# A hybrid decoder step on one core: the searches of a sparse list emitted further apart, and more products of ones ahead of the first wide product

## The chip, the cores and the metric

One Trainium2 chip, one of its cores. The metric is the device time of one launch in microseconds, the median of several runs; lower is better.

## The reference

One inference step of one decoder layer, for a prompt of 512 rows and a sample of 8 sequences with 4 rows each (544 rows of 1024 in all):

```
u = rmsnorm(h, g1);  h = h + 0.5 * rmsnorm(swiglu(u, wg, wu, wd), g2)
u = rmsnorm(h, g3);  z, xbc, dt, q, k, v, qi, ki, wi, g_ssd, g_att = split(u @ w_in)
y_ssd = ssd_branch(z, xbc, dt, ...)          # 32 heads in 8 groups
y_att = attn(q, k, v, qi, ki, wi)            # each row over its own 256 keys
merged = sigmoid(g_ssd) * (y_ssd @ w_br_ssd) + sigmoid(g_att) * (y_att @ w_br_att)
h = h + rmsnorm(merged @ w_out, g4)
...                                          # cross-attention to a memory, second FFN
```

The sparse attention of a sample row scores 4100 keys (4096 of them in paged caches), takes the 256 best, gathers their key and value rows by the page table, and attends over these:

```
score = einsum('bth,bths->bts', wi, relu(dots));  _, sel = top_k(score, 256)
k_sel = pool_k[page_table[sel // 128], sel % 128]   # and v_sel
```

## The kernel before

All work runs on one core, in float32. A wide product multiplies a weight block of 128 columns by 544 rows; operands are split into a high and a low part (`wh`, `wl` of a weight, `uh`, `ul` of the rows), and `mm` (line 315 issues them) makes three products for each of 8 blocks of k. `weights` loads a raw weight half by DMA (`wr`, three buffers), copies the high part on ScalarE (line 275) and subtracts for the low part on VectorE, or for some weights on GpSimd (line 276). There are two buffers each of `wh` and `wl`.

The kernel is written as generators. `weave` runs several of them by a clock of its own: a generator yields a pair (cost, delay), the cost moves that clock on, and the generator is resumed when its delay is over. This sets the order in which instructions are emitted. The framework then schedules them: the order of emission is their priority, and within each engine an instruction that isn't ready lets others pass. So the order on an engine can differ from that in the code.

**The start.** `load_x` loads the first 256 rows, and `first_T` transposes them on TensorE (line 481) for k = 0 to 7, two blocks of 128 rows each. ScalarE and VectorE make `uh` and `ul` of them (lines 485 and 486), with the first weight halves of the first FFN in between. Behind the transposes of k = 1, 3 and 5 `idle` multiplies a tile of ones by itself into a spare PSUM tile (line 248): 2, 2 and 8 products that nobody reads. Each leaves two records in the trace. Then the first wide products follow (line 315, `pgh`).

**The sparse list.** `sample_lists` finds the threshold of each sample row's list by 16 rounds of comparing and counting on VectorE, makes running counts, and then looks up the places of the 256 entries: 32 searches, each a `max_index` of 8 wanted counts in a row of 1028 (line 1130). They write slices of one tile and depend on nothing that the other generators do. It is begun beside the prompt's attention, and what is left of it goes on in `ssd`:

```python
fs.after(chain(rounds, self.sample_select(), call(sel_ex.close), self.sample_att()))
```

Here `rounds` is `sample_lists`; `sample_select` turns the places into row numbers (VectorE, one product); `sample_att` gathers key and value rows by indirect DMAs on GpSimd's queue, attends in four steps of 8 rows, and stores each step's result (`yas` to `yatt_d`, line 1712).

Beside that chain `ssd` weaves two more generators. `fronts` makes, group by group, the projections of B, C and x with their convolution (`ssd_x`, lines 1324 to 1341) and of z (`ssd_z`, line 1300); for two groups it also makes a piece of the gates, whose low parts GpSimd computes. When all groups are through it waits for the flag `fs`, which the end of `sample_att` sets; then `att_in` loads the attention's result (`yat`, line 1722) and splits it into `uh` and `ul`, and `att_out` multiplies it by `w_br_att`. `tails` runs `ssd_y` for each group: the scan, the state, and at its end the norm of the group (`rms`). There a sum of squares (line 346) goes through a chain of small VectorE operations for the reciprocal root (lines 331 to 336) to a diagonal `zt` (lines 357 and 359), which TensorE spreads over the rows (`psr`, line 360). Group g of `fronts` waits until the tail of group g - 2 has been emitted.

When `tails` and the chain have ended, `conv_rows` and `merge` follow: `merge` loads the 16 blocks of the branch's result (`yt`, three buffers, line 1758), splits them into `yh` and `yl`, weaves this with the rest of `att_out`, and multiplies by `w_br_ssd`.

Of the kernel before, what the change touches and what calls it, by code (L numbers as in the profile page):

```python
# [168 lines left out]
class Net:  # L169
# [297 lines left out]
    def first_T(self):  # L467


        nc, I = self.nc, self.I  # L470
        q = self.row_squares(0, (0,))
        pss = []
        for k in range(8):
            if k == 4:
                self.weights(("ffn1", "g", 0), [I["ffn1_wg"][0][:, :256]], 8)
            if k % 2 == 0:
                ps = self.ps1("pgx")
                pss.append(ps)
            v = ps[:, k % 2 * 256:(k % 2 + 1) * 256]
            for i in range(2):  # L480
                nc.tensor.transpose(v[:, i * P:(i + 1) * P], self.xin[i][:, k, :], self.ident)
            if k in (1, 3, 5):
                self.idle(self.spare, 2 if k < 5 else 8)
            gk = self.g1[:, k:k + 1]
            nc.scalar.activation(self.uh[:, k, :HA], v, AF.Copy, scale=gk)
            nc.vector.scalar_tensor_tensor(self.ul[:, k, :HA], v, gk, self.uh[:, k, :HA].bitcast(F32), op0=ALU.mult, op1=ALU.subtract)
        self.weights(("ffn1", "u", 0), [I["ffn1_wu"][0][:, :256]], 8)
        for i in range(2, 4):
            nc.sync.dma_start(self.xin[i], I["x_prompt"][0, i * P:(i + 1) * P, :].rearrange("p (k d) -> p k d", k=8))
        nc.sync.dma_start(self.xin[4], I["x_sample"].rearrange("b t (k d) -> (b t) k d", k=8))  # L490
        for c, ps in enumerate(pss):
            (nc.vector.tensor_copy if c % 2 else nc.scalar.copy)(self.hT[:, 2 * c:2 * c + 2, :HA], ps.rearrange("p (k t) -> p k t", k=2))

        def rest():
            self.row_squares(0, (1,), q)
            yield from self.row_factor(q, 0)

        return rest()
# [557 lines left out]
    def sample_lists(self):  # L1056
# [71 lines left out]
        nc.vector.tensor_scalar(at, at, bg, None, op0=ALU.subtract)  # L1128
        for r in range(32):
            nc.vector.max_index(self.IX[:, r * 8:(r + 1) * 8], at[:, r * 8:(r + 1) * 8], S)  # L1130
            yield 0.0, 3.4


    def gates(self, x, cs, tile):
# [960 lines left out]
```

## Time and profile before

| | |
|---|---|
| median of 3 runs | 2186.69 us (2183.43 to 2188.44) |
| the profiled execution's own time | 2168.1 us |
| its span, first to last instruction | 2165.3 us |
| mean granted TensorE clock | 0.981 |
| TensorE busy | 97% of the span |
| VectorE busy | 61% |
| ScalarE busy | 44% |
| GpSimd busy | 17% |

The profiled execution is one of its own, and every row below is from it. Busy time of an engine is the time in which it had an instruction in work. PEclk is the share of TensorE's full clock that was granted: 1.00 is 2.4 GHz and 0.50 is 1.2 GHz, and a value in between is a mean over a stretch that saw both.

### The profile page before, as it was taken

To read this page: it belongs to the slowest core of one execution; us is meant where nothing else is said; L and a number is where in the kernel's file an instruction comes from. 1 tells how busy PE (TensorE), PEld (TensorE's weight loads), DVE (VectorE), ACT (ScalarE), POOL (GpSimd) and SP (SyncE) were. 2 spreads that over 40 slices of the span, in tenths; PEclk is the share of its full clock that TensorE was granted. 3 is DMA by queue.
4 is the path that set the end of the run, shared out by engine and by line. 5 is a ranking of instruction groups with operands and counts; after the bars stand their busy time and mean duration, and the time that the engine had idled before them with its cause. 6 is when DMAs were issued, how large, how long until landed. Compare 5 with 4: busy or idle time off the path is not lost.

```text
span 2165.3 us, 41287 instructions
## 1 busy us (share of the span) xinstructions
PE 2096.3 (97%) x16725; PEld 1963.0 (91%) x16725; DVE 1324.1 (61%) x2759; ACT 956.2 (44%) x1821; POOL 377.7 (17%) x413
## 2 busy tenths in 40 slices
PE   8999999999999999999999999999999989999998
PEld 8999999998878769988889899899987889999998
DVE  6543334466587889997877788544663575424455
ACT  6323345345444675544555455323545443222233
POOL 0000011032113212205555620001210210000011
PEclk9999999998999899999999999999999989999999
DMA  6424556356443223444666556554444433233243
GB/s 200 130 68 137 154 183 230 104 145 197 139 145 93 75 81 105 137 140 140 177 184 184 163 160 194 175 163 168 155 143 156 140 109 117 78 108 90 72 133 101
DMA packets 320106, 301.70 MB, mean 139 GB/s; under 512 B 25416, under 2 KB 290632, under 8 KB 318868
## 3 DMA queue, kind: packets, MB, share of 16 engines
q1 hardware_dynamic: 310508, 272.58, 41.0%
q0 software_dynamic: 8448, 25.18, 3.9%
q8 instruction: 131, 2.15, 0.4%
q10 hardware_dynamic: 960, 1.31, 0.2%
q14 instruction: 59, 0.48, 0.1%
HBM read 261.14 MB, written 37.35 MB: 138 GB/s over the span
## 4 chain that ended last, share of the span: by engine, by line
PE 77%; DVE 12%; DMA 4%; ACT 4%; issue 2%; POOL 0%; SPq 0%; DVEq 0%; ACTq 0%; POOLq 0%
PE pg L315 44%; PE pgh L315 17%; PE pmo L601 2%; DVE wl L276 2%; DVE gtm L1087 1%; ACT wh L275 1%; DMA abc<-ac_d 1%; DMA yt<-yssd_d 1%; DMA wr<-in_ffn_wg 1%; DMA wr<-in_ffn_wu 1%; PE ph L1448 1%; PE pmkT L1821 1%; PE pqk L1199 1%; PE pmo L1888 1%; PE pms L1877 1%
## 5 line engine op out<-in xcount | busy, mean ns | idle before, releaser
L275 ACT CAST wh<-wr 128x1024 fp32r<-128x1024 f32 (+3 forms) x362 | 342.2, 959 | 510.7 <-PE pg L315 237.3
L276 DVE TENSOR_TENSOR wl<-wr,wh 128x1024 fp32r<-128x1024 f32 (+3 forms) x338 | 377.3, 1128 | 210.6 <-ACT wh L275 206.2
L315 PE MATMUL pg<-uh,wh 128*128 128x256 f32 (+1 forms) x2336 | 501.1, 295 | 0.0
L315 PE MATMUL pg<-uh,wl 128*128 128x256 f32 (+1 forms) x2336 | 490.6, 290 | 0.0
L315 PE MATMUL pg<-ul,wh 128*128 128x256 f32 (+1 forms) x2336 | 489.7, 290 | 0.0
L315 PEld LDWEIGHTS pg<-uh,wh 128*128 128x128 f32 x2336 | 378.4, 190 | 19.4 <-issue 16.6
L315 PEld LDWEIGHTS pg<-ul,wh 128*128 128x128 f32 x2336 | 378.8, 190 | 3.0 <-issue 2.6
L315 PEld LDWEIGHTS pg<-uh,wl 128*128 128x128 f32 x2336 | 378.0, 189 | 1.3 <-issue 1.0
L315 PE MATMUL pgh<-uh,wh 128*128 128x288 f32 (+2 forms) x880 | 260.6, 299 | 6.4 <-ACT wh L275 4.3
L315 PE MATMUL pgh<-uh,wl 128*128 128x256 f32 (+2 forms) x880 | 259.8, 298 | 4.2 <-DVE wl L276 4.2
L315 PE MATMUL pgh<-ul,wh 128*128 128x256 f32 (+1 forms) x880 | 257.0, 294 | 0.0
L315 PEld LDWEIGHTS pgh<-uh,wh 128*128 128x128 f32 (+1 forms) x880 | 170.3, 195 | 9.9 <-ACT wh L275 5.1
L315 PEld LDWEIGHTS pgh<-uh,wl 128*128 128x128 f32 (+1 forms) x880 | 169.8, 194 | 7.6 <-DVE wl L276 6.6
L315 PEld LDWEIGHTS pgh<-ul,wh 128*128 128x128 f32 x880 | 171.3, 195 | 1.2 <-issue 0.8
L375 POOL TENSOR_TENSOR sqf<-sqf,sqt 128x256 f32<-128x256 f32 (+1 forms) x48 | 54.5, 1135 | 529.2 <-ACT sqt L374 517.3
L315 PE MATMUL pgh<-hh,wh 128*128 128x288 f32 (+1 forms) x352 | 101.8, 289 | 0.0
L315 PE MATMUL pgh<-hl,wh 128*128 128x288 f32 (+1 forms) x352 | 101.2, 288 | 0.0
L315 PE MATMUL pgh<-hh,wl 128*128 128x288 f32 (+1 forms) x352 | 101.0, 287 | 0.0
L1336 DVE SCALAR_TENSOR_TENSOR XO<-CB,convw,XO 128x600 f32<-128x600 f32 x96 | 82.8, 863 | 13.7 <-ACT XO L1334 13.1
L627 DVE TENSOR_TENSOR g<-pg,rt 128x544 f32<-128x544 f32 x32 | 23.2, 725 | 100.5 <-PE pg L315 100.5
L630 DVE TENSOR_TENSOR g<-pg,g 128x544 f32<-128x544 f32 x32 | 23.2, 725 | 97.7 <-PE pg L315 97.7
L712 POOL DMA_INDIRECT G<-in_cache_kidx,ix x16 | 16.8, 1053 | 362.5 <-DVE ix L707 282.3
(608 smaller groups left out, 3840.4 us busy)
## 6 DMA issues: line engine op xcount, KB each, us to landing
wr<-in_w_in SPq DMA_DIRECT2D x66, 512.0 KB
wr<-in_ffn_wg SPq DMA_DIRECT2D x48, 512.0 KB
wr<-in_ffn_wu SPq DMA_DIRECT2D x48, 512.0 KB
wr<-in_ffn_wd SPq DMA_DIRECT2D x44, 384.0 KB
wr<-in_ffn_wd SPq DMA_DIRECT2D x44, 320.0 KB
kt_d<-KT SPq DMA_DIRECT2D x8, 1024.0 KB
KT<-kt_d SPq DMA_DIRECT2D x16, 512.0 KB
wr<-in_w_in SPq DMA_DIRECT2D x32, 256.0 KB
```

The costliest lines, as they stand in the source:

```text
L275: nc.scalar.copy(hi[:, s], r)
L276: (lo_eng or nc.vector).tensor_tensor(lo[:, s], r, hi[:, s].bitcast(F32), op=ALU.subtract)
L315: nc.tensor.matmul(o, a[:, k, c0:c0 + m], x[:, r0:r0 + n], start=(k == 0 and j == 0), stop=(k == KT - 1 and j == 2))
L375: (nc.vector if last else nc.gpsimd).tensor_tensor(acc[:, :n], acc[:, :n], s[:, :n], op=ALU.add)
L601: nc.tensor.matmul(ps[:, :256], a[:, k, i * P:(i + 1) * P], b[:, k, :], start=(k == 0 and j == 0), stop=(k == 7 and j == 2))
L627: nc.vector.tensor_tensor(g1[:, :n], pg, rt[:, sl], op=ALU.mult)
L630: nc.vector.tensor_tensor(g1[:, :n], pu, g1[:, :n], op=ALU.mult)
L1087: nc.vector.scalar_tensor_tensor(G, S, thr[:, j:j + 1], one, op0=ALU.is_ge, op1=ALU.mult, accum_out=cnt[:, j:j + 1])
L1199: nc.tensor.matmul(ps[:, :W], qT[hb:hb + 64, h // 2, i * P:(i + 1) * P], ks[hb:hb + 64, gp, :W], start=True, stop=True)
L1336: nc.vector.scalar_tensor_tensor(xo, CB[:, j:j + 600], cw(j), xo, op0=ALU.mult, op1=ALU.add)
L1448: nc.tensor.transpose(ps[:, b * P:(b + 1) * P], h0[n // 2][:, n % 2 * 4 + b, :], self.ident)
L1821: nc.tensor.transpose(ps[:, (z * 2 + i) * P:(z * 2 + i + 1) * P], mk[:, i, (k + z) * P:(k + z + 1) * P], self.ident)
```

## The change

Behind the transposes of k = 5 there are 18 products of ones in place of 8. Behind each of the 32 searches the generator asks `weave` for a delay of 4.6 in place of 3.4.

```diff
@@ first_T
             if k in (1, 3, 5):
-                self.idle(self.spare, 2 if k < 5 else 8)
+                self.idle(self.spare, 2 if k < 5 else 18)
@@ sample_lists
         for r in range(32):
             nc.vector.max_index(self.IX[:, r * 8:(r + 1) * 8], at[:, r * 8:(r + 1) * 8], S)
-            yield 0.0, 3.4
+            yield 0.0, 4.6
```

## Rows read from the trace of the kernel before

**Rows 1.** The page: busy time, share of the span and instructions of the engines.

```profile
PE 2096.3 (97%) x16725; PEld 1963.0 (91%) x16725; DVE 1324.1 (61%) x2759; ACT 956.2 (44%) x1821; POOL 377.7 (17%) x413
```

**Rows 2.** Stretches of the start: length, busy time of each engine, PEclk, DMA.

```profile
12.30:15.00 2.70, 0.00 (x0) 0.00 (x0) 2.70 (x5) 2.70 (x6) 0.00 (x0) 1.00 0.84 275
...
16.20:19.40 3.20, 3.20 (x17) 3.20 (x16) 3.10 (x6) 3.20 (x7) 0.00 (x0) 0.50 1.05 341
```

**Rows 3.** TensorE in order of time: start, duration, instruction, idle time before it.

```profile
9.69 1.50 PE L248 MATMUL spare<-ones 128*128 128x128 f32 x12
11.03 0.38 PE L481 MATMUL pgx<-ident,y 128*128 128x128 f32 x2
...
11.91 0.38 PE L481 MATMUL pgx<-ident,y 128*128 128x128 f32 x2
15.03 0.39 PE L315 MATMUL pgh<-uh,wh 128*128 128x256 f32 x1 [2.74 <-ACT wh L275]
```

**Rows 4.** ScalarE in order of time, at the start.

```profile
13.93 1.05 ACT L275 CAST wh<-wr 128x1024 fp32r<-128x1024 f32 x1
```

**Rows 5.** Line 1130: duration in ns (least, median, most), first and last start.

```profile
L1130 DVE FIND_INDEX8 eqm<-ct,S x32: 1210/1224/1233, 831.4 to 948.3; 128x8 uint32<-128x1028 f32 x32
```

**Rows 6.** TensorE's waits, 820 to 1000 us: total, times, longest.

```profile
PE psr L360 <- DVE zt L357: 5.8, 2, 3.3
```

**Rows 7.** Stretches around the two waits, columns as in the stretches above.

```profile
920.00:930.00 10.00, 7.50 (x54) 6.53 (x53) 10.00 (x20) 0.63 (x1) 1.18 (x1) 1.00 0.45 133
980.00:990.00 10.00, 6.69 (x47) 5.90 (x46) 10.00 (x32) 2.56 (x4) 1.21 (x2) 0.94 0.35 98
990.00:1000.00 10.00, 10.00 (x58) 9.00 (x56) 6.32 (x16) 3.09 (x4) 1.67 (x3) 0.71 0.22 71
```

**Rows 8.** VectorE in order of time, in three chains of the reciprocal root.

```profile
914.81 0.15 DVE L331 TENSOR_SCALAR nw<-nw 128x5 int32<-128x5 int32 x1
...
928.10 0.66 DVE L357 TENSOR_TENSOR zt<-ident,nw 128x512 f32<-128x512 f32 x1
...
976.20 2.39 DVE L1574 CAST pgf<-pgi 128x256 f32<-128x256 uint32 x1
978.51 2.37 DVE L331 TENSOR_SCALAR nw<-nw 128x5 int32<-128x5 int32 x1
...
1369.42 0.17 DVE L331 TENSOR_SCALAR nw<-nw 128x5 int32<-128x5 int32 x1
...
1371.42 0.69 DVE L357 TENSOR_TENSOR zt<-ident,nw 128x512 f32<-128x512 f32 x1
```

**Rows 9.** VectorE by line, 914.8 to 928.9 us: busy us, mean ns.

```profile
L1130 DVE FIND_INDEX8 eqm<-ct,S 128x8 uint32<-128x1028 f32 x7 | 8.5, 1210 | 0.0
```

**Rows 10.** GpSimd in order of time, low halves of gate weights.

```profile
907.38 5.30 POOL L276 TENSOR_TENSOR wl<-wr,wh 128x1024 fp32r<-128x1024 f32 x2
...
975.95 4.91 POOL L276 TENSOR_TENSOR wl<-wr,wh 128x1024 fp32r<-128x1024 f32 x2 [0.48 <-ACT wh L275]
```

**Rows 11.** SP's queue in order of time: issues of DMAs.

```profile
1285.20 0.38 SPq L1712 DMA_DIRECT2D yatt_d<-yas  x1
...
1315.54 3.67 SPq L1722 DMA_DIRECT2D yat<-yatt_d  x8
...
1386.50 1.30 SPq L1758 DMA_DIRECT2D yt<-yssd_d  x3
```

**Rows 12.** ScalarE in order of time, first cast of the attention's result.

```profile
1318.36 0.65 ACT L323 CAST uh<-yat 128x544 fp32r<-128x544 f32 x1
```

**Rows 13.** TensorE in order of time, last products of `ssd_z`.

```profile
1318.77 0.41 PE L315 MATMUL pg<-uh,wl 128*128 128x256 f32 x2
```

**Rows 14.** One stretch, line 315 alone: length, TensorE's busy time, PEclk.

```profile
1319.00:1335.00 16.00, 10.99 (x81) 1.00 0.36 130
```

**Rows 15.** Stretches of the loading in `merge`, columns as in the stretches above.

```profile
1390.00:1430.00 40.00, 34.12 (x230) 31.91 (x231) 21.18 (x28) 15.51 (x23) 0.00 (x0) 0.91 0.65 212
...
1390.00:1400.00 10.00, 7.55 (x37) 7.24 (x38) 6.02 (x8) 4.70 (x8) 0.00 (x0) 0.66 0.71 218
```

## The prediction, made before the changed kernel was run

> **What bounds the kernel now.** I read the page's busy times first: TensorE is busy for 2096.3 of the 2165.3 us [rows 1], so an edit can win only where TensorE waits or where its clock is down. Then I took the two places that the diff touches, asking of each which wait ends last.
>
> *The start.* The stretches of the first 20 us [rows 2] show TensorE with nothing to do from 12.3 to 15.0 us, at a granted clock of 1.00, while ScalarE is busy for all of those 2.70 us; and from 16.2 to 19.4 us TensorE is busy throughout at a granted clock of 0.50, which is 1.2 of 2.4 GHz. TensorE's order of time [rows 3] gives the gap its ends: the last pair of transposes starts at 11.91 and takes 0.38 us (12.29), and the first wide product starts at 15.03 after 2.74 us, released by ScalarE's copy of a weight half, which runs from 13.93 to 14.98 [rows 4]. So the gap has two prices: the wait, which ScalarE sets, and the clock that falls behind it, 3.2 us at half speed, 1.6 us of work.
>
> *The searches.* The 32 searches take 1.22 us of VectorE each and lie between 831.4 and 949.5 us [rows 5]. The chain of TensorE's waits between 820 and 1000 us has one name that counts: `psr` (line 360) waits twice for `zt` (line 357), 5.8 us in all, 3.3 us at most [rows 6]. By stretches [rows 7] VectorE is busy for 10.00 of 10 us around both waits, TensorE loses 2.50 us from 920 to 930 and 3.31 us from 980 to 990, and after the second the clock is 0.94 and 0.71 over two tens of us, (0.06 + 0.29) x 10 = 3.5 us of work. In all 2.5 + 3.3 + 3.5 = 9.3 us can be had here.
>
> What makes `zt` late is seen in VectorE's order of time [rows 8]: the chain of small operations from line 331 to line 357 takes 2.0 us where nothing stands between its steps (1369.42 to 1371.42), and 13.3 us at the first wait (914.81 to 928.10), with seven whole searches of 1.21 us in between, 8.5 us [rows 9].
>
> **The change part by part.** *More products of ones* (18 for 8 behind the transposes of k = 5). Twelve records of such products, six products, take from 9.69 to 11.03 us, 0.112 us a record [rows 3]. Ten more products are 20 records, 2.23 us. If they run in the gap they end at 12.29 + 2.23 = 14.52, before the release at 14.98, so the wait itself keeps its length and the first product keeps its time; the price is nothing while ScalarE's copy covers it, and up to 2.23 us if it didn't. What is left idle is 0.5 us, and I expect no fall of the clock behind it: gain 1.6 us, and I take 1.5 because TensorE's waits further on could take back a little. Bounds: a gain of nothing (the clock falls all the same) and a loss of 0.6 us: the scheduler sets TensorE's order and already put the eight products among transposes. Were the new ones put ahead of the pair at 11.03, all that ScalarE does from the copies of `uh` behind them to 14.98 would move by 2.23 us, less the 1.6 us.
>
> *Searches further apart.* Nothing is added or removed: 32 x 1.2 = 38.4 us of the weave's own clock are put between the searches, and all that follows in their generator, `sample_select` and `sample_att` with its DMAs on the queues of SP and POOL, is emitted that much later against `fronts` and `tails`. From the first start to the last they took 948.3 - 831.4 = 116.9 us [rows 5] for 31 x 3.4 = 105.4 us of delays, a ratio of 1.11, so 38.4 us are at most 43 us of the trace. Two things follow.
>
> First, between 914.81 and 928.10 fewer searches should stand in the chain. At one per 3.8 us (116.9 / 31) that stretch of 13.3 us would hold 3.5, and it holds 7; at one per 5.1 us (4.6 x 1.11) it would hold 2.6, or 5.2 if they crowd in as before. That is 1.8 to 4.4 searches less, 2.2 to 5.3 us, ahead of a `psr` that waited 2.5 us. I take 2.3 us of gain and leave the second wait as it is. Bounds: 9.3 us gained (both go, with the clock), and 6.8 us lost (one more wait like the second, 3.3 us, with its 3.5 us of clock), since searches now also lie where `sample_select` was.
>
> The second wait I leave because VectorE's rows have another cause for it: line 331's operation, 0.17 us at 1369.42, takes 2.37 us at 978.51, and the cast ahead of it 2.39 us [rows 8]. Meanwhile GpSimd computes two low halves of weights, 4.91 us from 975.95, as it did from 907.38 for 5.30 us, shortly ahead of the first chain [rows 10]. The Trainium skill, SBUF — State Buffer, section Who interferes with whom, has the rule: GpSimd shares a pair of ports with VectorE, and for certain operations whoever starts first holds it for a whole instruction while the other blocks. By that rule alone both waits are GpSimd's and stay, and the gain below would be 2.3 us smaller; the stretched operations agree with it, the seven searches in the chain speak for the other reading.
>
> Second, the end of the branch. The last store of `sample_att` is issued at 1285.20 and the loads that wait for all of them at 1315.54 [rows 11]: 30 us of slack, of which a store's way out takes some, for a move of 38 to 43 us. With 40 us the store goes out at 1325.2. A load needs at most 2.8 us to the first cast of `uh`, at 1318.36 [rows 12]; with as much for the store, the first cast is at 1330.8 and, with 1.3 us for the two halves of `uh` and `ul`, the first product of `att_out` at about 1332, where the last products of `ssd_z` end at 1319 [rows 13]: 13 us without wide products. From 1319 to 1335 these hold 10.99 of TensorE's 16.00 us [rows 14], so the tail gives it 5.0 us to do in that time, and 13 - 5 = 8 us would be idle. They are paid back: `att_out` also covers the loading of `yt`, which the tail of the last group releases and not `att_out` (issued from 1386.50 [rows 11]). There TensorE is idle for 40 - 34.12 = 5.9 us and loses 3.4 us more by a clock of 0.66 [rows 15], 9.3 us. Products that end 8 us later fill them: 8.0 - 9.3 = -1.3 us. Bounds: 11.5 us lost (nothing paid back, and a fall of the clock for 3.5 us as after the second wait), and 9.3 us gained (the tail alone fills the 13 us).
>
> Sum: -1.5 - 2.3 - 1.3 = -5.1 us against the profiled execution's own 2168.1 us. That execution is 18.6 us below the median of the runs shown, 2186.69; I carry the difference over: 2181.6 us.
>
> **The rivals.** *A, the searches are filler.* The scheduler hands VectorE whatever is ready when nothing earlier is, wherever it was emitted. For it: seven in one chain are twice what their spacing gives, so a chain with gaps may draw them at any spacing, and GpSimd's hold of VectorE stays. Against it: had they filled every gap from the start, their 39 us would hardly have lasted until 949. Then only the start gains: 2186.7 - 1.5 = 2185.2 us; likewise if the order moves but the waits merely change places.
>
> *B, `att_in` comes late and isn't paid back.* Place: 1319 to 1332 us. It decides if the last store of `sample_att` is issued after about 1313 us (1315.5 less the way out), a move of over 28 us, and the loads of `yt` start later too because the last tail doesn't run ahead. Price 8.0 us, 11.5 with the clock: 2186.7 - 1.5 + 8.0 = 2193.2 us, up to 2196.7. Against it: the tail has VectorE and ScalarE more to itself then, without the casts of `att_in`, and may run ahead.
>
> *C, both waits go*, and the clock with them, since `sample_select` also leaves the second chain: -1.5 - 9.3 - 1.3 = -12.1, 2174.6 us. Against it: GpSimd's two halves.
>
> **How the numbers follow.** A fifth of a per cent, 4.4 us, is about what a measurement can tell from no change. My forecast gets 0.36, A 0.34, B 0.20, C 0.10. Forecast and C are faster by more than that (0.46), A is the same (0.34), B is slower (0.20). Alone the forecast would lie between 2177 and 2184 us. For 8 in 10 the range reaches from C to just short of B's price: 2173.5 to 2192.5 us.
>
> **What would show it.** Right: no gap over 1 us before the first wide product, and a clock of 1.00 from 15 to 22 us; no wait of `psr` near 925, and fewer than seven searches in that chain; the searches' last start near 990; the last store of `sample_att` near 1325; the idle time moved from 1390-1430 to 1319-1332. Wrong: searches that still end near 950 (A); TensorE idle for 8 us ahead of `att_out` and again while `yt` loads (B); transposes of the start that stand behind the new products.

## The result, and the profile after

The changed kernel takes 2202.85 us (median of 7 runs, 2199.78 to 2208.99), the kernel before beside it 2186.99 us (7 runs, 2183.43 to 2196.14). The ratio is 1.0078, with an interval of 1.0062 to 1.0095: slower by 0.8%, 15.9 us between the medians, where 5 us less had been forecast.

The profiled execution after took 2202.85 us by itself, the median. The one of before took 2168.1 us, 18.6 us under its median, so the two pages exaggerate the difference. A second profile of before (run e0_before below) took 2185.56 us and stands for it in what follows. The page after, busy times as in [rows 1]:

```profile
PE 2116.9 (96%) x16745; PEld 1972.1 (90%) x16745; DVE 1319.0 (60%) x2759; ACT 959.1 (44%) x1821; POOL 372.3 (17%) x413
```

Twenty records more on TensorE are the ten products of ones. The start, in the stretches of [rows 2]:

```profile
12.30:15.00 2.70, 2.53 (x23) 2.29 (x22) 2.70 (x5) 2.70 (x5) 0.00 (x0) 1.00 0.86 262
16.20:19.40 3.20, 3.20 (x29) 3.20 (x28) 2.69 (x5) 2.95 (x7) 0.00 (x0) 1.00 1.07 326
```

TensorE is now idle for 0.17 us of the first stretch, and in the second it runs at a granted clock of 1.00 where it had 0.50. This part did what it should.

The searches after (line 1130, as in [rows 5]), and TensorE's waits for `zt` from 820 to 1000 us (as in [rows 6]):

```profile
L1130 DVE FIND_INDEX8 eqm<-ct,S x32: 1208/1225/1234, 824.0 to 946.2; 128x8 uint32<-128x1028 f32 x32
```

```profile
PE psr L360 <- DVE zt L357: 5.6, 2, 2.9
```

The searches take 122.2 us from the first start to the last, where they took 116.9. The delays between them grew by 35%, their real distance by 5%; and in the second profile of before, with the old delay, they took 121.6 us (830.4 to 952.0), so that against it the distance did not grow. Both waits of `psr` are still there. What did move is the end of the chain, on SP's queue (compare [rows 11]):

```profile
1274.51 0.37 SPq L1712 DMA_DIRECT2D yatt_d<-yas  x1
...
1359.91 0.54 SPq L1712 DMA_DIRECT2D yatt_d<-yas  x1
...
1362.83 3.81 SPq L1722 DMA_DIRECT2D yat<-yatt_d  x8
```

The last store of `sample_att` goes out at 1359.91, 74.7 us later than in the first profile of before and 53.2 us later than in the second (1306.68). What TensorE does around it, in order of time:

```profile
1354.61 0.41 PE L315 MATMUL pg<-uh,wl 128*128 128x256 f32 x2
1354.86 1.02 PE L1423 MATMUL pst<-xe,Bt 128*128 128x256 f32 x4
1357.53 0.30 PE L1707 MATMUL poT<-ident,od 128*128 128x128 f32 x1 [1.65 <-DVE od L1703]
...
1366.21 0.66 PE L1491 MATMUL pfin<-ident,H 128*128 128x128 f32 x2
1367.64 1.28 PE L315 MATMUL pg<-uh,wh 128*128 128x256 f32 x4 [0.77 <-ACT uh L323]
```

The wide products of `ssd_z` end at 1355.02 and those of `att_out` begin at 1367.64: 12.6 us with small products alone, nearly all of them the last group's. This is the place that the prediction had named (1319 to 1332, 13 us). TensorE is busy for 8.76 of these 12.62 us, at a granted clock of 0.94.

To count what a stretch costs I take its length less busy time times granted clock (idle time, and time lost by the clock). The three stretches below are the second last group of `tails` and the last one, each up to the store of its result, and then `merge` up to the first load of the weight behind it (`w_out`). Columns as in [rows 7], after:

```profile
1277.71:1348.15 70.44, 64.21 (x528) 53.90 (x527) 44.01 (x100) 32.93 (x71) 28.05 (x36) 0.93 0.47 142
1348.15:1406.63 58.48, 54.61 (x433) 49.58 (x432) 41.13 (x98) 18.77 (x33) 0.00 (x0) 0.94 0.55 168
1406.63:1500.10 93.47, 88.62 (x694) 86.24 (x692) 41.28 (x51) 30.96 (x43) 0.00 (x0) 1.00 0.57 176
```

and the same stretches in the second profile of before:

```profile
1288.32:1346.65 58.33, 58.12 (x506) 53.96 (x505) 49.15 (x108) 33.92 (x72) 9.13 (x17) 1.00 0.59 189
1346.65:1397.94 51.29, 51.26 (x432) 47.68 (x431) 39.53 (x88) 15.06 (x27) 0.00 (x0) 1.00 0.48 140
1397.94:1486.88 88.94, 82.40 (x624) 80.26 (x623) 37.55 (x47) 28.20 (x40) 0.00 (x0) 0.96 0.56 176
```

Lost are 10.7, 7.1 and 4.9 us after, against 0.2, 0.0 and 9.8 us before. GpSimd's column says what differs in the first of them: the gathers of the fourth step (busy for 28.05 us in place of 9.13) now lie beside the second last group. That they cost the 10.7 us isn't shown by it (see e7_nolast, which has as many there and loses nothing). The loads of `yt` in `merge` moved too, after and in the second profile of before:

```profile
1420.42 1.27 SPq L1758 DMA_DIRECT2D yt<-yssd_d  x3
```

```profile
1407.89 1.30 SPq L1758 DMA_DIRECT2D yt<-yssd_d  x3
```

Counted from the store of the second last group (1348.15 and 1346.65) they start after 72.3 us in place of 61.2.

### The profile page after: what moved, and what is told of

Its sections match the earlier page's. It is cut to its first block, busy times and chain, and to the rows that moved or that the text cites. A ratio compares the mean times of both kernels' runs of the same rounds, so it can differ in the third digit from the quotient of the medians.

```text
span 2201.0 us, 41334 instructions
## 1 busy us (share of the span) xinstructions
PE 2116.9 (96%) x16745; PEld 1972.1 (90%) x16745; DVE 1319.0 (60%) x2759; ACT 959.1 (44%) x1821; POOL 372.3 (17%) x413
## 4 chain that ended last, share of the span: by engine, by line
PE 76%; DVE 12%; DMA 4%; ACT 4%; issue 2%; another core or an unknown queue 0%; POOL 0%; SPq 0%; DVEq 0%; ACTq 0%; POOLq 0%
PE pg L315 44%; PE pgh L315 16%; DVE wl L276 2%; PE pmo L601 2%; DVE gtm L1087 1%; ACT wh L275 1%; DMA wr<-in_ffn_wu 1%; DMA yt<-yssd_d 1%; DMA wr<-in_ffn_wg 1%; PE pmkT L1821 1%; PE pmo L1888 1%; PE pY L1511 1%; PE pkT L1654 1%; DVE XO L1336 1%; PE pst L1423 1%
## 5 line engine op out<-in xcount | busy, mean ns | idle before, releaser
L1628 POOL DMA_INDIRECT kv<-in_cache_k,slot x64 | 72.6, 1134 | 47.4 <-PE pkT L1654 24.0
```

Of the source, the lines that this page charges most:

```text
L1628: nc.gpsimd.indirect_dma_start(out=t[:, hf, :], out_offset=None, in_=(pk, pv)[x], in_offset=off)
```

## The experiments

Five groups of runs, each on one chip with the kernel before beside it. The medians of before were 2186.9 (A), 2167.8 (B), 2182.8 (C), 2185.4 (D) and 2165.9 us (E), so chips differ by 1%, and only ratios within a group are compared. "Late" is the move of `sample_att` in the delays of `weave`; the next columns are the last store on SP's queue and the first cast of `uh` from the attention's result less the start of the last `zt` of `ssd_z` on ScalarE.

| run | group | late | last store | cast less `ssd_z` | ratio (95%) |
|---|---|---|---|---|---|
| changed kernel | | 38.4 | 1359.9 | +10.9 | 1.0078 (1.0062 to 1.0095) |
| e0_before | A | 0 | 1306.7 | -0.9 | 1.0000 (0.9985 to 1.0015) |
| e1_ones | A | 0 | 1303.0 | -1.0 | 0.9989 (0.9973 to 1.0005) |
| e2_apart | A | 38.4 | 1359.5 | +11.2 | 1.0083 (1.0054 to 1.0112) |
| e3_pause | A | 38.4 | 1362.9 | +10.5 | 1.0086 (1.0062 to 1.0110) |
| e4_half | B | see below | 1283.6 | -0.9 | 1.0001 (0.9991 to 1.0012) |
| e5_compress | B | 38.4 at the start | 1312.8 | +0.5 | 1.0070 (1.0055 to 1.0084) |
| e6_early | B | see below | 1218.5 | -0.8 | 1.0017 (1.0005 to 1.0028) |
| e7_nolast | B | 38.4 | 1335.4 | +11.2 | 1.0022 (1.0009 to 1.0034) |
| e8_after | C | 38.4 | 1348.6 | +10.6 | 1.0075 (1.0056 to 1.0093) |
| e9_b_nolast | C | see below | 1298.8 | -6.8 | 1.0016 (1.0003 to 1.0029) |
| e10_b_compress | C | 0 | 1287.3 | -0.9 | 1.0081 (1.0064 to 1.0099) |
| e11_d43 | C | 28.8 | 1328.0 | +1.5 | 1.0015 (1.0003 to 1.0026) |
| e12_lastlate | D | 38.4, step 4 alone | 1352.3 | +13.4 | 1.0063 (1.0040 to 1.0085) |
| e13_after_cover | D | 38.4 | 1352.8 | +24.2 | 1.0089 (1.0061 to 1.0117) |
| e14_ones_cover | D | 0 | 1295.5 | +27.1 | 0.9990 (0.9972 to 1.0008) |
| e15_ones | D | 0 | 1301.1 | -0.8 | 0.9986 (0.9971 to 1.0000) |
| e16_last19 | E | 19.2, step 4 alone | 1309.1 | -1.5 | 0.9991 (0.9981 to 1.0001) |
| e17_ones_gates | E | 0 | 1280.0 | -1.5 | 1.0011 (1.0001 to 1.0021) |

**Which of the two edits.** e0_before is the kernel before. e1_ones and e15_ones have the first edit alone, e2_apart the second alone, and e3_pause leaves the searches as they were and puts the same 38.4 behind them:

```diff
-            yield 0.0, 3.4
+            yield 0.0, 3.4 if r < 31 else 41.8
```

> The kernel before, unchanged, for a second profile: the first one was 18.6 us below the median of its runs. Every theory expects a ratio of 1.000. If the 18.6 us are chance of that one execution, this span is near 2184 us, and the rows in which it differs from the first show what the kernel before also loses in a usual execution; the difference of the two profiles at hand (35.7 us of span) then overstates the loss of 16 us.

> Only the 18 products of ones; the searches keep their delay of 3.4. Theory L (all of the loss comes from sample_att, which begins 40 us later): the gap of the start is filled, the granted clock stays at 1.00 from 15 to 22 us, and the kernel is 1 to 2 us faster than before, a ratio of 0.9995. Rival O (any edit reshuffles the order that the scheduler writes, and the result of that is what was measured): the order of later stages moves too, and the time differs from before by several us in either direction.

> Only the 18 products of ones once more, for a narrower interval together with e1_ones: 0.9985 to 1.0 by the 1.5 us that I had worked out (0.0007 of the time), 1.000 if the clock's fall cost nothing in the end.

> Only the delay of 4.6; the start keeps 8 products of ones. Theory L: slower than the kernel with both edits by 1 to 2 us, a ratio to before of 1.008 to 1.009, first gather near 1041 us and TensorE idle in many small pieces from 1060 to 1360 us. Rival O: a ratio well away from 1.008, on either side.

> The searches keep 3.4, and one delay of 41.8 stands behind the last of them, so that sample_select and sample_att are emitted 38.4 later, as in the changed kernel, with the searches as near to each other as before. Theory L: ratio 1.008, the first gather near 1041 us, the last store of sample_att near 1360. Rival S (the spacing of the searches costs, because their VectorE time now lies elsewhere): 1.000 to 1.002.

The products of ones gain: 2186.9 x 0.0011 = 2.4 us and 2185.4 x 0.0014 = 3.1 us, with intervals that reach up to no change. All of the loss is the other edit's (1.0083), and e3_pause has it whole (1.0086) with the searches no further apart. So the spacing neither costs nor gives; what costs is that `sample_att` is emitted 38.4 later.

**Why it starts so late.** e11_d43 has both edits with a delay of 4.3 at the searches, and e8_after is the changed kernel beside it.

> The changed kernel again, beside the kernel before on one chip, so that its rows and those of the runs beside it can be compared. Every theory: 1.006 to 1.009, the first gather 35 to 42 us later than in before, the product for the row numbers (pslot) 35 to 40 us late though its operand is ready within 8 us of before's time.

> Both edits with a delay of 4.3 at the searches alone: 28.8 of the 38.4. Theory R (the product for the row numbers takes a buffer of the ring of four in PSUM, which are handed out in the order of emission, so that it moves from one gap between the tail's users to the next): the first gather is near before's time or near the changed kernel's, nothing between, and the ratio 0.999 to 1.001 or 1.007 to 1.009 with it. Rival G (the gathers move in proportion): 28 to 32 us later than before, ratio 1.003 to 1.006.

In e11_d43 the first gather starts at 1033 us, in e8_after at 1038, in the second profile of before at 1004: 29 and 34 us of move (against another chip's profile, since before has none on chip C) for delays of 28.8 and 38.4. That is the move in proportion that rival G expected, not one of R's two places. But both had tied the loss to that start, G at 0.3% or more, and it is nearly gone (1.0015 against 1.0075 on one chip). So a late start by itself isn't what costs; the last store tells the two apart, at 1328.0, ahead of the last products of `ssd_z`, and at 1348.6, behind them. In the changed kernel VectorE, TensorE and GpSimd show what the start waits for:

```profile
1004.97 0.42 DVE L1582 TENSOR_TENSOR row<-row,own 128x256 f32<-128x256 f32 x1
```

```profile
1035.94 0.53 PE L1587 MATMUL pslot<-ct,row 128*128 128x32 f32 x4
```

```profile
1040.73 1.03 POOL L1628 DMA_INDIRECT kv<-in_cache_k,slot  x1 [0.47 <-issue]
```

The row numbers are ready at 1005.4, and the product that needs them runs 30.5 us later. That it stands behind the tail's users of a ring of PSUM buffers is a reading of the code; no run here tried it.

**The last step alone.** e12_lastlate and e16_last19 are the kernel before with one delay ahead of the fourth step (38.4 and 19.2); nothing ahead of that step is moved.

```diff
         for st in range(4):
+            if st == 3:
+                yield 0.0, 38.4
```

> The kernel before, with one delay of 38.4 ahead of the fourth step of sample_att: its searches, its choice and its first three steps stay where they were, and only the last step is emitted late. Theory W (the loss is att_in's wait for the last store, once that comes behind the last products of ssd_z): the first gather near before's 1001 to 1004 us, the last store near 1340 to 1350, behind the end of ssd_z, and most of the loss is there, ratio 1.005 to 1.008. Rival P (the loss lies beside all four steps, which are shifted against the groups): 1.000 to 1.002.

> As e12_lastlate, with 19.2 in place of 38.4 ahead of the fourth step. Theory W, with its threshold: the last store moves by some 20 us from 1307 and still comes ahead of the end of ssd_z (1341 in the second profile of before), so that nothing is lost, 0.999 to 1.002. A rival without a threshold (each us of lateness costs its share): half of e12_lastlate's 0.63%, 1.003.

The late fourth step alone makes 0.63% of the 0.8, half of the delay makes nothing (on a chip of another sort, see below, so that the threshold rests on e11_d43 as well). The stretches of e12_lastlate and, below them, of e15_ones on the same chip:

```profile
1273.00:1338.00 65.00, 61.03 (x522) 51.68 (x521) 42.34 (x99) 32.26 (x71) 29.97 (x36) 0.97 0.48 146
1338.00:1399.00 61.00, 56.54 (x441) 50.84 (x440) 42.94 (x98) 18.97 (x33) 0.00 (x0) 0.92 0.55 169
1399.00:1496.00 97.00, 91.10 (x699) 88.53 (x698) 41.61 (x53) 30.94 (x43) 0.00 (x0) 0.98 0.56 170
```

```profile
1283.00:1341.00 58.00, 57.96 (x505) 53.80 (x504) 48.76 (x106) 33.59 (x71) 9.04 (x17) 1.00 0.59 190
1341.00:1392.00 51.00, 51.00 (x431) 47.59 (x429) 39.55 (x88) 15.06 (x27) 0.00 (x0) 1.00 0.47 138
1392.00:1482.00 90.00, 83.35 (x628) 80.80 (x627) 37.74 (x49) 28.57 (x41) 0.00 (x0) 0.96 0.57 177
```

Lost are 5.8 + 9.0 + 7.7 = 22.5 us against 0.0 + 0.0 + 10.0 = 10.0: 12.5 us, beside a difference of 16.2 us between the two medians (2198.8 and 2182.59). The same sum for e2_apart and e0_before (chip A) is 3.3 + 7.8 + 9.6 = 20.7 against 0.2 + 0.0 + 9.8. The place behind `ssd_z` costs 8 to 9 us, the one beside the fourth step 3 to 6, and `merge` gives back 0.3 to 2.3.

On chip C the same sum doesn't find the loss. The stretches of e8_after and, below them, of e11_d43:

```profile
1270.00:1337.00 67.00, 62.86 (x541) 52.46 (x541) 44.91 (x102) 32.58 (x71) 29.29 (x36) 0.99 0.51 150
1337.00:1393.00 56.00, 52.23 (x433) 47.23 (x432) 41.27 (x98) 19.10 (x34) 0.00 (x0) 1.00 0.58 175
1393.00:1487.00 94.00, 88.47 (x688) 85.70 (x688) 40.73 (x51) 30.78 (x43) 0.00 (x0) 1.00 0.57 174
```

```profile
1266.00:1336.00 70.00, 66.49 (x592) 57.57 (x591) 50.38 (x113) 36.03 (x76) 26.05 (x35) 1.00 0.58 171
1336.00:1391.00 55.00, 54.24 (x450) 50.04 (x448) 41.61 (x92) 17.70 (x31) 0.00 (x0) 1.00 0.52 158
1391.00:1482.00 91.00, 83.36 (x622) 81.55 (x621) 37.09 (x47) 27.94 (x39) 0.00 (x0) 0.94 0.55 172
```

Lost are 4.8 + 3.8 + 5.5 = 14.1 us in e8_after and 3.5 + 0.8 + 12.6 = 16.9 in e11_d43, whose median is 11.1 us lower. The profiled execution of e8_after is the fastest of its six (2190.2 us), 6.7 under their median, and its clock didn't fall behind the gap: the stretch with the gap costs 3.8 us there.

**Taking the wait away.** e7_nolast (both edits) and e9_b_nolast (the kernel before, meant as its control) store the fourth step's result to a scratch tensor and fill its columns with zeros:

```diff
+        nc.sync.dma_start(self.yatt_d[:, :, TP + 24:TP + 32].rearrange("k p t -> p k t"), zy)
...
-            nc.sync.dma_start(self.yatt_d[:, :, TP + st * 8:TP + (st + 1) * 8].rearrange("k p t -> p k t"), yas)
+            to = self.yatt_d[:, :, TP + st * 8:TP + (st + 1) * 8] if st < 3 else self.yas_d
+            nc.sync.dma_start(to.rearrange("k p t -> p k t"), yas)
```

> Both edits, but the fourth step's result goes to a scratch tensor, and its eight columns of yatt_d are filled with zeros ahead of the first step: att_in no longer waits for the last store, while every step is computed and emitted where it was. It leaves the last eight sample rows without their attention. Theory E has two parts: the hole ahead of att_out (7.1 us lost from 1348 to 1407 in the changed kernel) and the groups beside the fourth step (10.7 us from 1278 to 1348). This run takes away the first alone: 4 to 7 us of the 16 come back, ratio 1.004 to 1.006. If only the wait of att_in were the cost, all comes back, 1.000; if it is nothing, 1.008 stays.

> The kernel before with the fourth step's result sent to scratch as in e7_nolast, so that att_in doesn't wait for it: the control of that run. Theory W (in the changed kernel most of the loss is att_in's wait for the last store, which in before had come in time): nothing is gained here, ratio 0.999 to 1.001, since the last store is issued some 30 us ahead of the loads. If this run gains 0.3% or more as well, what e7_nolast won back came from another order and not from the wait.

This did not do what it was for. SP's queue in e7_nolast:

```profile
1335.42 0.54 SPq L1717 DMA_DIRECT2D yas_d<-yas  x1
1336.01 1.22 SPq L1437 DMA_DIRECT2D E<-ac_d  x2
1337.34 0.52 SPq L272 DMA_DIRECT2D wr<-in_w_br_att  x1
1337.96 2.46 SPq L1727 DMA_DIRECT2D yat<-yatt_d  x5
```

The loads need nothing of that store any more, and still stand behind it on the queue; the gap of wide products is there as before, from 1330.5 to 1343.4. The loss is only 0.22% nevertheless. The chip, group B's, may be the reason. The stretches of e7_nolast, as above:

```profile
1262.50:1323.50 61.00, 60.89 (x543) 51.64 (x543) 45.04 (x101) 32.47 (x71) 30.86 (x36) 1.00 0.55 165
1323.50:1382.50 59.00, 54.63 (x431) 49.78 (x430) 40.99 (x97) 18.72 (x33) 0.00 (x0) 0.94 0.54 166
1382.50:1476.00 93.50, 89.32 (x698) 86.78 (x696) 41.56 (x53) 30.98 (x43) 0.00 (x0) 1.00 0.58 177
```

Here 0.1 + 7.6 + 4.2 = 11.9 us are lost, in e4_half on the same chip 2.3 + 0.0 + 8.9 = 11.2: the gap costs what it costs on A and D, but `merge` gives 4.7 us back, and the stretch beside the fourth step loses nothing. On TensorE the waits that nothing in the profile releases, called issue, come to 0.0 us from 990 to 1410 in every profile of groups B and E, and to 9.9 us in the changed kernel, 9.7 in e2_apart and 2.6 in e0_before. The changed kernel itself was not run on a chip of that sort, so whether the chip or the scratch tensor makes the difference isn't shown. e9_b_nolast is 0.16% slower than before, but it isn't a clean control: its edit also put 3.4 in place of 4.6 behind the 16 rounds and the running counts (lines 1088 and 1104), which takes 17 x 1.2 = 20.4 off ahead of the searches, as in the other doses below. What each part does to its time is open.

**Denser steps.** e5_compress (both edits) and e10_b_compress (the kernel before) shorten the eight delays within each step, to end the late chain in time:

```diff
-                yield 1.6, 4.0
+                yield 1.6, 2.8
...
-                yield 0.8, 4.0
+                yield 0.8, 2.8
```

> Both edits, and the eight delays of 4.0 in each of the four steps of sample_att are 2.8: 32 x 1.2 = 38.4 taken out again behind the searches. sample_att begins 40 us late as in the changed kernel and should end near where it did, the last store near 1310 to 1320. Theory E: the loss goes, ratio 0.999 to 1.002, and the last two groups of tails lose under 2 us in place of 17.8. Rival P: the loss stays, 1.005 or more, since three of the four steps lie as late as before and are now denser.

> The kernel before with the eight delays of 4.0 in each step of sample_att at 2.8, the control of e5_compress. Theory W: the denser steps cost by themselves, since TensorE waited 11.7 us for gathers in e5_compress where before had no such wait; ratio 1.004 to 1.008, and e5_compress then says nothing on the end of the chain. Rival P (the four steps lie badly against the groups): the denser steps cost nothing at before's place, 0.999 to 1.001.

The control loses as much by itself (1.0081, though on another chip), so e5_compress can't speak on the late end; in e5_compress TensorE waits for gathers:

```profile
PE pO L1698 <- DMA kv<-in_cache_v,slot: 8.3, 5, 3.2
PE pkT L1654 <- DMA kv<-in_cache_k,slot: 3.4, 3, 2.7
```

**Other doses.** e4_half and e6_early put 4.0 and 2.2 in place of 4.6 throughout the generator, and so also behind the 16 rounds and the running counts (lines 1088 and 1104), which the expectations overlooked: 17 x 0.6 and 17 x 2.4 come off ahead of the searches.

```diff
-            yield 0.0, 4.6
+            yield 0.0, 4.0
```

> Both edits, but a delay of 4.0 in place of 4.6: half of the 38.4. Theory E (the end is late: the fourth step of sample_att runs into the last groups and into att_out's place, and nothing is lost while its last store still comes ahead of the last products of ssd_z): the last store comes 19 to 22 us later than in the second profile of before (1306.7), near 1327, still ahead of the end of ssd_z (1341 there); nothing is lost, ratio 0.999 to 1.001. Rival P (what counts is how the four steps fall against the groups of tails, 67 to 77 us each): about half of the loss, 1.004, or a value on no line between 1.000 and 1.008.

> Both edits, but with a delay of 2.2: the searches nearer to each other and sample_att up to 38 us earlier than in the kernel before. Theory E: the end has still more slack, which is worth nothing: ratio 0.998 to 1.000 (the start's 1 to 2 us), if VectorE can take the searches. Rival P: any value, up to 1.008. If VectorE is too full beside the end of the prompt's attention, psr waits longer there, 3 us or more.

e4_half moves the chain by 19.2 - 10.2 = 9.0, its last store is at 1283.55, no later than in [rows 11], so that it doesn't try a later end; its time is that of before: searches at 4.0 gain nothing either (`psr` waits 6.7 us, 3.7 at most). e6_early starts the gathers near 933 us and loses 0.17%; an earlier chain gained nothing here. With a delay of 2.2 the searches do draw together: 74.2 us from the first start to the last (813.5 to 887.7).

**Wide products for the gap.** e13_after_cover (both edits) and e14_ones_cover (the first edit) move the second piece of gates behind `ssd_z` of group 7; e17_ones_gates puts it behind `att_in`, where its products multiply the attention's rows in place of the input's.

```diff
-                if g in (1, 2):
-                    yield from self.gates(1, (g + 1,), lambda: ...
+                if g in (1, 7):
+                    yield from self.gates(1, (2 if g == 1 else 3,), lambda: ...
```

> Both edits, and the second of the two pieces of gates in fronts, two columns of wide products which wait for no step of sample_att, stands behind ssd_z of group 7 and ahead of the wait for the flag, in place of behind group 2. Theory W: these products stand in the place where TensorE had nothing wide to do until the attention's result came; most of the loss goes, ratio 0.999 to 1.002. Rival P: the loss stays at 1.006 to 1.009.

> The 18 products of ones, the searches at 3.4, and the second piece of gates moved behind group 7, as in e13: the control of that run, and a version that might beat both. Theory W: there is no hole to cover here, so that the move gains nothing but the second wait of psr near 985 us, if GpSimd's low halves are its cause (up to 3 us): 0.997 to 1.000. If it is slower than before, the covered run beside it carries that price too.

> The 18 products of ones, the searches at 3.4, and the second piece of gates behind att_in and ahead of att_out, so that att_in isn't delayed as it was in e14_ones_cover and the piece's wide products stand beside the end of the last group and the loading of yt. In e14_ones_cover the stretch of that loading lost 1.7 us where e15_ones lost 9.9, and the group ahead of it 6.5 where e15_ones lost nothing, because the load of yat came 15 us later. If that delay was all of the 6.5 us, this run is 6 us faster than e14_ones_cover, 0.995 to 0.998 of before. If the piece is missed more where it was, behind group 2 (8 us lost in the groups after it in e14_ones_cover), 0.999 to 1.001.

The cover fails (its two values in the table's fifth column are high because `att_in` is emitted behind the piece). In e13_after_cover the last store is issued at 1352.84 and the loads of `yat` only at 1372.64, behind the piece. So the gap wasn't filled but moved: the piece's products end at 1367.48, those of `att_out` begin at 1377.46. The piece may also be missed where it was:

```profile
1049.00:1128.00 79.00, 69.61 (x566) 58.45 (x565) 48.38 (x118) 35.49 (x74) 37.23 (x46) 0.91 0.49 142
```

That group loses 15.7 us, where e2_apart lost 8.1 on chip A.

e14_ones_cover shows something else. Its last store is early (1295.48), but the loads of `yat` stand behind the piece, and it has a gap without wide products nearly as long as the changed kernel's, from 1348.31 to 1359.26. Its stretches:

```profile
1276.00:1334.00 58.00, 56.70 (x493) 52.32 (x493) 47.88 (x100) 30.91 (x65) 14.92 (x19) 1.00 0.50 153
1334.00:1392.00 58.00, 54.81 (x432) 50.28 (x431) 40.04 (x90) 20.18 (x36) 2.73 (x2) 0.94 0.52 157
1392.00:1486.00 94.00, 92.33 (x730) 90.75 (x728) 42.72 (x54) 30.21 (x42) 0.00 (x0) 1.00 0.61 187
```

Lost are 1.3 + 6.5 + 1.7 = 9.5 us, no more than the 10.0 of e15_ones: `merge` gives 8.3 back, which is the payback that the prediction had counted on, and the time is that of before. So such a gap, here behind the piece, need not cost. e14_ones_cover is no faster than e15_ones beside it, and e17_ones_gates is 0.11% slower than before. The products of ones alone have the lowest ratios here, 0.9986 and 0.9989.

## Why the prediction was wrong

*The base.* The 18.6 us between the profiled execution and the median were carried over as chance. They are more likely the difference of two sorts of chip: 2165.9 and 2167.8 us against 2182.8 to 2186.9. Which chip the first profile is from isn't known, but its time and its lack of issue waits are those of groups B and E.

*The start, -1.5.* Right, mechanism and sign: no gap, no fall of the clock, and a gain of 2.4 and 3.1 us in two runs whose intervals just include none.

*The first wait of `psr`, -2.3.* Wrong. The searches were taken to spread with their delays; VectorE took them when it was free, as rival A said. The last one starts at 946.2 in place of the 990 expected (948.3 and 952.0 in the two profiles of before), six stand in the chain in question (seven before), and the waits add up to 5.6 us as they did to 5.8. The second wait was left as it is, rightly: the cast of line 1574 beside GpSimd's low halves, which took 2.39 us [rows 8], takes 2.51 us in the changed kernel, where it starts with the second of them (974.77 to 977.17). In e4_half the same cast comes just ahead of GpSimd's start and takes 0.30, and the operation that falls beside it takes 2.09 us in place of 0.41 at the next such step:

```profile
970.76 0.30 DVE L1574 CAST pgf<-pgi 128x256 f32<-128x256 uint32 x1
...
972.15 2.09 DVE L1577 TENSOR_TENSOR row<-row,dum 128x256 f32<-128x256 f32 x1
```

```profile
971.57 4.94 POOL L276 TENSOR_TENSOR wl<-wr,wh 128x1024 fp32r<-128x1024 f32 x2 [0.44 <-ACT wh L275]
```

That is the rule that the prediction took from the Trainium skill, SBUF — State Buffer, section Who interferes with whom: GpSimd and VectorE share a pair of ports, and for certain operations the one that starts first holds it for a whole instruction while the other blocks. The traces agree, with 2.51 us against 0.30 and 2.09 against 0.41.

*The end of the branch, -1.3: the step that failed.* The payback failed. The prediction let `att_out` end 8 us later into a loading of `yt` that stays where it is, and set 9.3 us of idle time and clock there against 8.0 lost in the gap. The loading didn't stay. From the store of the second last group to the loads of `yt` it is 72.3 us in the changed kernel against 61.2 before, 75.0 against 60.9 on D (e12_lastlate and e15_ones), 72.5 against 60.8 on B (e7_nolast and e4_half): 11 to 14 us more. In the changed kernel 7.2 of its 11.0 lie in the last group's tail (58.5 in place of 51.3 us). So the stall moved along with the products that were to fill it. Of the 9.3 us, 4.9 came back in the changed kernel's own profile, 0.3 on chip A, 2.3 on D, 4.7 on B, 7.1 on C (e8_after beside e11_d43). The 9.3 is also a little high: by the measure used here [rows 15] give 40 - 34.12 x 0.91 = 9.0.

The other terms fared differently. The move was put at 38 to 43 us; on one chip the last store moved by 52.8 (1306.7 to 1359.5). The gap of 13 us without wide products came out at 12.6. The 8.0 us to be lost in it seem to have come out too, at 7.1 in the changed kernel's own profile and 7.6 to 9.0 on A, B and D, but that is luck. The tail gave TensorE 8.76 us to do and not 5.0, so that it was idle for 3.9 to 4.5 us in that stretch; the rest is the clock (0.92 to 0.94 over it), which the prediction had priced apart, at 3.5 us, and only in the bound. And one term was missing: the second last group, beside the fourth step, loses 3.3 us (A), 5.8 (D) and 10.7 (the changed kernel's own profile), where before had 0.2 or less. On C it is 4.8 against 3.5, and on B, with the same gathers beside it, 0.1.

So rival B was right on the place and on the late loads of `yt`, and too low on the price: it ended at 2186.7 - 1.5 + 11.5 = 2196.7 us.

B set the point from which it decides at a move of 28 us. On one chip the loss goes from 0.15% to 0.75% between delays of 28.8 (e11_d43) and 38.4 (e8_after); by the rows it is where the last store falls behind the last products of `ssd_z`.

*What stays open.* That a fourth step emitted late enough costs is shown, by e12_lastlate, which moves nothing else, and by e11_d43 against e8_after. By what it costs isn't. The gap alone doesn't explain it: e7_nolast has it whole and loses 0.22%, e14_ones_cover has one and is no slower than before, and no run took it out of a kernel that loses. The stretches account for 10.6 of 18.1 us on chip A, for 12.5 of 16.2 on D and for nothing on C; the four groups ahead of them (991 to 1284 us) lose 23.4 us in e2_apart against 19.0 in e0_before, and the rest I couldn't place. Each of these sums is from one execution of each kernel. What the issue waits are isn't settled, nor whether the changed kernel loses 0.8% or 0.2% on chips without them.

## What to carry to other kernels

A longer delay between instructions that depend on nothing need not spread them: here they ran when their engine was free, and what moved was all that is emitted behind them. So price such an edit by the end of its chain: what is the last transfer needed for, and which wide work ends just ahead of it. And before a gap is written off as paid back by a later stall, check that the stall stays where it is when the gap opens; here what ended it moved by 11 us as well.

## What was not expected of the hardware

Chips differ for this kernel by 1% (each was used in one session, so that chip and session can't be told apart), and not evenly: in the stage with the gathers TensorE loses 19.0 us in four groups (e0_before, 995 to 1288), where the first profile loses 2.2 (995 to 1288). In that stage alone TensorE has waits without a releaser on the slower chips, some of them in the middle of a run of like products. The rows of e0_before:

```profile
1020.18 0.41 PE L1457 MATMUL pys<-hT__11166,CZ 128*32 128x128 f32 x3 [0.16 <-issue]
1020.88 0.42 PE L1457 MATMUL pys<-hT__11166,CZ 128*32 128x128 f32 x3 [0.29 <-issue]
1022.32 0.38 PE L1457 MATMUL pys<-hT__11166,CZ 128*32 128x128 f32 x2 [1.02 <-issue]
```

Eight products with the same two operand tiles come in three pieces. No such row stands in the first profile of before between 1000 and 1082 us.
